# Opening a kernel's attention stage two products before its projections end

## The chip, the cores and the metric

The kernel runs on one core of a Trainium2 chip. The metric is the time of one execution on the device, in microseconds (us). A core has five engines that run their own instruction queues in order and wait for one another by semaphores: TensorE (PE in the profile; PEld is its weight load), VectorE (DVE), ScalarE (ACT), GpSimd (POOL) and SyncE (SP, which here only issues DMAs). TensorE writes its sums into PSUM, a small memory of eight banks; the other engines work from SBUF, the large on-chip memory, and carry the sums out of PSUM.

## The reference

One layer of a transformer trunk on 2048 tokens of width 1024, in float32:

```
h = rms_norm(x, g_pre_mix)
q, k, v = split_heads(h, w_qkv)                      # 16 heads of 64
for each chunk c of 64 tokens:                       # sees its own chunk and the 8 before
    sc  = q_c @ k_band^T / 8 + bias                  # bias: learned, clipped relative position
    o_c = softmax(sc) @ v_band
x = x + rms_norm(merge(o) @ w_o, g_post_mix)
h = rms_norm(x, g_pre_ffn)
x = x + rms_norm((silu(h @ w_gate) * (h @ w_up)) @ w_down, g_post_ffn)
```

## The kernel before

**Numbers.** Each float32 operand of a dense product is split into a rounded part ("hi") and the rest ("lo"), and three matmuls stand for one product (`products`, L197 to L199). ScalarE makes hi by a copy that rounds, VectorE makes lo by a subtraction (`split`, L356 and L357).

**Projections.** `project` (L1333) works in two groups `g` of 1024 tokens. Each dense product is a block scheme with seven products instead of eight, named in the order B11, B21, T1, T2, B22, T3, T4 (`BLOCKS`). In each group come first the values (`values_of`), then the queries and keys (`queries_keys`), four times (`c`) seven products of 24 matmuls, each product in two halves `i` (0 is the queries' half, 1 the keys'). In `values_of`, `put` adds a sum from PSUM to a stored term on VectorE (L1241), and `emit_v` (L426) scales the result by its token's inverse root on ScalarE (L428) and stores it. In `queries_keys`, the closing of a half is a sum on VectorE (L1305) and `emit_qk` (L431): a multiplication by the row of inverse roots (L436, VectorE), the hi part (L438, ScalarE), the lo part (L439, VectorE), and the stores to DRAM on SP.

**Scratch.** hi and lo take their tiles from `narrow`, which is `scratch` (L238): four tiles of 512 columns in a pool that always lives (`xp`) and, while the projections' pool `fp` is open, three more (`tmp`), in turn. A tile that still waits for its store to land holds up whoever takes it next. Tiles named `hb0` to `hb6` hold a group's block operands (`hb_tile`); in the second group `hb0` holds T3's operand.

**Attention.** 32 jobs `Attend(n, p)`: a quarter of 512 tokens `n` (in the order 1, 0, 2, 3) and a pair of heads `p`, with four slots of 128 queries each. A slot is: `scores` (L517), matmuls into the banks `st` (L533, L534), one reduction of each head on VectorE that adds the bias and finds the row's minimum (L542), one exponential on ScalarE (L546); `scaled` (L552), a reciprocal on VectorE and a multiplication by it on GpSimd (L558); `transposed` (L562), eight transposes on TensorE (L573) and copies out (L576 on VectorE, L578 on ScalarE); `fifth` (L587, L588). A job ends with `output`, the product with the values (L603). Scores run three slots ahead of transposes (`AHEAD`). The first quarter's eight jobs run alone; later ones have dense products between their slots. Job 0's operands are loaded during the projections (after T1 of the last `c`) into `hb2` and `hb3`; each later job has a `load` of its own on SP: two DMAs of queries, two of keys, four of biases, and for every second job two of values, into tiles of the pool `ap`. Job `j + 2` loads when the last scores of job `j` have been issued.

**Places and order.** `fp` and the projections' six PSUM banks (`psf`) are closed after the last product, and the attention's pools `ap`, `psa` and `pss` are opened on the same memory; two more banks (`ps`, tag `mm`) live throughout, and the first quarter's transposes use them. TensorE's order is the program's own; on the other engines the framework's planner chooses an order beforehand, by priority and by its own estimate of when each operand is ready, and each queue then runs in that order. `last_pool` and `last_sp` chain the DMAs of `weight_sums` (L842), which builds sums of weights in DRAM for the feed-forward part, behind the latest instruction of the queue that they go to: copies on SP (L852), accumulating DMAs on GpSimd (L856).

The transition, before the change:

```
drain()
stack_f[0].close()
... # ap, psa, pss opened; first_banks()
with tc.high_priority(offset=300):
    jobs[1].load()
for t in range(AHEAD):
    ahead(t)                    # scores of slot t
    if t < AHEAD - 1:
        jobs[0].scaled()
```

Of the kernel before, what the change touches and what calls it, by code (L numbers as in the profile page):

```python
# [9 lines left out]
F32 = mybir.dt.float32  # L10
F32R = mybir.dt.float32r
# [6 lines left out]
P = 128  # L18
# [31 lines left out]
def trunk(  # L50
# [195 lines left out]
    def narrow(name):  # L246
        return scratch(name)[:, :HALF]
# [156 lines left out]
    bias = {}  # L404

    bias_bufs = []

    def bias_tile(n, h, t=None):

# [13 lines left out]
            )  # L423
        return t

    def emit_v(n, m, u, t):  # L426

        act.activation(t, t, AF.Copy, scale=rs[n][:, m : m + 1])  # L428
        sp.dma_start(v_d[n][:, m, u * HALF : u * HALF + HALF], t)

    def emit_qk(n, p, which, src, t=None):  # L431

        scale = (0.125, 1.0)[which]
        if t is None:
            t = narrow("t")
        dve.tensor_tensor(t, src, rows_of[n], op=ALU.mult)  # L436
        hi, lo = (narrow(m).bitcast(F32R) for m in ("hi", "lo"))
        act.activation(hi, t, AF.Copy, scale=scale)  # L438
        dve.scalar_tensor_tensor(lo, t, scale, hi.bitcast(F32), op0=ALU.mult, op1=ALU.subtract)  # L439
        for a, part in enumerate((hi, lo)):  # L440
            part = part.bitcast(F32)
            if which == 0:
                sp.dma_start(q_d[n][p][:, a, :], part)
                continue
            for h, own in enumerate(heads):
                sp.dma_start(k_d[n][p][heads[a], h, :], part[own])
# [787 lines left out]
    def values_of(g, b, big):  # L1234

        s0, s1 = 2 * g, 2 * g + 1
        p1, z = ([big[:, 4 * n + m, :] for m in range(4)] for n in range(2))

        def put(n, m, u, a, b_, op=ALU.add):
            t = narrow("v")  # L1240
            dve.tensor_tensor(t, a, b_, op=op)  # L1241
            emit_v(n, m, u, t)

        def after(name, m, pt):
            if name == "B11":
                act.activation(p1[m], pt, AF.Copy)
            elif name == "B21":
                put(s0, m, 0, pt, p1[m])
            elif name == "T1":
                act.activation(z[m], pt, AF.Copy)  # L1250
            elif name == "T2":
                dve.tensor_tensor(p1[m], p1[m], pt, op=ALU.subtract)
                dve.tensor_tensor(z[m], z[m], p1[m], op=ALU.add)
            elif name == "B22":
                put(s1, m, 0, pt, z[m])
            elif name == "T3":
                dve.tensor_tensor(p1[m], pt, p1[m], op=ALU.subtract)
                put(s1, m, 1, pt, z[m], ALU.subtract)
            else:
                put(s0, m, 1, pt, p1[m])  # L1260

        for name in BLOCKS:
            b.need(name)
            w = [front.take() for _ in range(2)]
            begin = g == 0 and name == "B11"
            for part in [range(4)] if begin else [range(2), range(2, 4)]:
                pts = {m: bank("pv") for m in part}
                for m, k in [(m, k) for k in range(4) for m in part] if begin else [(m, k) for m in part for k in range(4)]:
                    tok = slice(m * P, m * P + P)
                    hi, lo = (t[:, k % 2 * HALF : k % 2 * HALF + HALF] for t in w[k // 2])  # L1270
                    products(pts[m], b.t[name][:, 0, k, tok], b.t[name][:, 1, k, tok], hi, lo, k == 0, k == 3)
                    yield 3 * C512
                    if k == 3:
                        after(name, m, pts[m])

    def queries_keys(g, b, big, after):

        def product(pts, name, first, then):
            hi, lo = front.take()
            for i in range(2):  # L1280
                for k in range(4):
                    c = slice(i * HALF + k * P, i * HALF + k * P + P)
                    products(
                        pts[i], hi[:, c], lo[:, c], b.t[name][:, 0, k, :], b.t[name][:, 1, k, :],
                        first and k == 0, k == 3, not first,
                    )
                    yield 3 * C512
                then(i)

        for c in range(NPAIR // 2):  # L1290
            at = 6 * (c % 2)
            p1, u2 = ([big[:, n + i, :] for i in range(2)] for n in (at, 4))
            p5 = [big[:, (2, 8)[c % 2] + i, :] for i in range(2)]
            s0, s1 = 2 * g, 2 * g + 1

            def copy(pts, dst):
                return lambda i: act.activation(dst[i], pts[i], AF.Copy)

            def u(i):
                dve.tensor_tensor(u2[i], p1[i], pb[i], op=ALU.subtract)  # L1300
                dve.tensor_tensor(p5[i], p5[i], p1[i], op=ALU.add)

            def closing(pts, terms, n, p, op=ALU.subtract):
                def go(i):
                    dve.tensor_tensor(terms[i], pts[i], terms[i], op=op)  # L1305
                    emit_qk(n, p, i, terms[i], terms[i])

                return go

            pa, pc = ([bank(n) for _ in range(2)] for n in ("pa", "pc"))  # L1310
            pb = []

            def t2():
                pb.extend(bank("pb") for _ in range(2))
                return pb

            steps = (
                ("B11", lambda: pa, True, copy(pa, p1)),
                ("B21", lambda: pa, False, lambda i: emit_qk(s0, 2 * c, i, pa[i])),
                ("T1", lambda: pc, True, copy(pc, p5)),  # L1320
                ("T2", t2, True, u),
                ("B22", lambda: pc, False, closing(pc, u2, s1, 2 * c, ALU.add)),
                ("T3", lambda: pb, False, closing(pb, p5, s1, 2 * c + 1)),
                ("T4", lambda: pb, False, closing(pb, p1, s0, 2 * c + 1)),
            )
            for name, pts, first, then in steps:
                yield from product(pts(), name, first, then)
                if c == NPAIR // 2 - 1:
                    after(name)

# [2 lines left out]
    def project():  # L1333
# [71 lines left out]
        for g in range(NG):  # L1405
            if g:
                big = xp.tile([P, 10, HALF], F32, tag="big", name="terms", bufs=1)
            yield from values_of(g, groups[g], big)
            drain()
            if g == 0:  # L1410
                later.extend(pause(20.0) + roots_by_tokens(2, 10.0, 12.0) + pause(8.0) + roots_by_tokens(3, 10.0, 12.0))

            def after(name, g=g):
                if g + 1 == NG:
                    if name == "T1":
                        jobs[0].load(True)
                    return
                if name == "B11":
                    now(build(1, "L11") + build(1, "L12"))
                elif name == "B21":  # L1420
                    now(build(1, "L21") + build(1, "L22"))
                elif name == "T1":
                    later.extend(timed((0.5, build(1, "B11", 1.8))))
                elif name == "T4":
                    later.extend(timed(
                        (0.5, build(1, "B21", 2.2)), (11.0, build(1, "T1", 2.5)), (24.0, build(1, "T2", 4.0)),
                        (42.0, build(1, "B22", 2.5)), (53.0, build(1, "T4", 2.5)), (64.0, build(1, "T3", 2.0)),
                    ))

            yield from queries_keys(g, groups[g], big, after)  # L1430

    def ffn():

# [115 lines left out]
    ctx.enter_context(tc.manual_schedule(engines={mybir.EngineType.PE}))  # L1549

    jobs = [Attend(n, p) for n in SEQ_OF for p in range(NPAIR)]
    open_ffn(0)
    sums_, done = weight_sums(), 0.0
    for c in project():
# [2 lines left out]
        if 350.0 < done and done % 8.0 < 1.0:  # L1557
            next(sums_, None)
    drain()
    stack_f[0].close()  # L1560
    phase.clear()

    phase["ap"] = stack_a.enter_context(tc.tile_pool(name="ap", bufs=2, reuse_waits="tile"))
    phase["psa"] = stack_a.enter_context(tc.tile_pool(name="psa", bufs=2, space=PSUM, reuse_waits="tile"))
    phase["pss"] = stack_s.enter_context(tc.tile_pool(name="pss0", bufs=2, space=PSUM, reuse_waits="tile"))
    first_banks()
    lates = [Late(o_d[n], POST_MIX, x[n], x1_d[n], n) for n in range(NQ)]
    work, owed, left = iter(()), [0.0], [0.0]

# [11 lines left out]

    slots = 4 * len(jobs)
    per = slots // NQ
    AHEAD = 3

    def ahead(t):
        if t == per:
            later_banks()
# [2 lines left out]
            if t % 4 == 3 and t // 4 + 2 < len(jobs):  # L1591
                jobs[t // 4 + 2].load()

    with tc.high_priority(offset=300):
        jobs[1].load()
    for t in range(AHEAD):
        ahead(t)
        if t < AHEAD - 1:
            jobs[0].scaled()
    for t in range(slots):  # L1600
        share = left[0] / max(per - t % per - 1, 1)
        if t > 0 and t % 4 == 0:
# [126 lines left out]
```

## Time and profile before

| | us |
|---|---|
| three timed runs | 2382.28, 2382.46, 2384.13; median 2382.46 |
| the profiled execution | 2379.12 |
| its span, first to last instruction | 2377.4 |
| TensorE busy in the span | 2325.9 (98%) |
| VectorE, ScalarE, GpSimd busy | 1636.7, 1149.6, 317.5 |
| end of the projections in the span | 476.45 |
| first output product of the attention | 501.82 |

A row of a timeline gives the start and the duration in us, the engine, the line of the kernel, the operation and its tiles (out<-in), the shape, and how many instructions were merged (x); in brackets stands how long the engine was idle before it, and what released it. Matmuls overlap their neighbours, so the distance between starts is what one costs. A row of a windows view gives, for a stretch of the span, its length, then each engine's busy time with its number of instructions, the clock granted to TensorE (1.00 is full), the share of time in which the DMA engines were busy, and GB/s. A row of a line's or tile's view gives minimum, median and maximum duration in ns and the first and last start. A row of DMA issues gives the number of issues, the size of one, and the median us from issue to landing; such rows here are from the window 440 to 500.

### The profile page before, as it was taken

How to read it: one execution, taken by the hardware profiler on the slowest of the kernel's cores; microseconds unless marked ns; L12 is line 12 of the kernel's file. 1: busy time of each engine (PE TensorE's matmuls, PEld its weight loads, DVE VectorE, ACT ScalarE, POOL GpSimd, SP SyncE). 2: the span in 40 equal slices, each digit the busy share in tenths (PEclk: the TensorE clock that was granted, in tenths of full speed). 3: DMA queues.
4: the chain of work that ended last, by engine and by line, in shares of the span. 5: the costliest groups of instructions: out<-in, count | busy, mean ns of one | idle time of the engine just before them, and what ended most of it. 6: DMA issues, size and time to landing. Idle time of an engine off the chain costs nothing.

```text
span 2377.4 us, 32908 instructions
## 1 busy us (share of the span) xinstructions
PE 2325.9 (98%) x11456; PEld 1908.3 (80%) x11456; DVE 1636.7 (69%) x2620; ACT 1149.6 (48%) x2031; POOL 317.5 (13%) x422
## 2 busy tenths in 40 slices
PE   8999999989999999999999999999999999999998
PEld 7888888878777777778888888888888888888886
DVE  7787856667566665669787877677667676555577
ACT  7544643367666565666333343455343333334454
POOL 1000011134333433420100000000000000000002
PEclk9999999999999999999999999999999999999999
DMA  8777899988897788765976463567665657447654
GB/s 298 255 254 264 246 276 270 288 235 225 220 257 214 248 253 239 227 226 204 288 262 210 158 213 138 186 221 248 221 217 190 221 162 234 149 158 244 193 187 148
DMA packets 231509, 531.80 MB, mean 224 GB/s; under 512 B 26512, under 2 KB 42912, under 8 KB 226864
## 3 DMA queue, kind: packets, MB, share of 16 engines
q1 hardware_dynamic: 219440, 482.52, 63.7%
q0 software_dynamic: 11904, 47.19, 7.0%
q8 instruction: 90, 1.47, 0.3%
q14 instruction: 75, 0.61, 0.1%
HBM read 382.23 MB, written 170.44 MB: 232 GB/s over the span
## 4 chain that ended last, share of the span: by engine, by line
PE 70%; DVE 2%; ACT 1%; issue 1%; DMA 0%; POOL 0%; DVEq 0%
PE pd L199 6%; PE pd L197 6%; PE pd L198 6%; PE pb L197 5%; PE pb L199 5%; PE pb L198 5%; PE tt L603 4%; PE pa L199 3%; PE pa L197 3%; PE pa L198 3%; PE pc L197 3%; PE pc L199 3%; PE pc L198 3%; PE tt L573 2%; PE mm L199 2%; PE mm L197 2%
## 5 line engine op out<-in xcount | busy, mean ns | idle before, releaser
L558 POOL TENSOR_SCALAR sc<-sc,rows 128x640 f32<-128x640 f32 (+4 forms) x256 | 194.9, 774 | 311.2 <-DVE rows L555 142.1
L546 ACT ACTIVATE sc<-sc,rows 128x640 f32<-128x640 f32 (+4 forms) x256 | 193.1, 757 | 75.9 <-DVE rows L542 75.0
L197 PE MATMUL pb<-hb,w_wg_T 128*128 128x512 f32 x528 | 205.9, 390 | 0.3
L199 PE MATMUL pb<-hb,w_wg_T 128*128 128x512 f32 x528 | 205.4, 389 | 0.0
L198 PE MATMUL pb<-hb,w_wg_T 128*128 128x512 f32 x528 | 205.4, 389 | 0.0
L542 DVE CUSTOM_DVE_ANT_0 sc<-st,bias 128x640 f32<-128x640 f32 (+2 forms) x248 | 174.6, 733 | 38.1 <-PE st L534 22.7
L533 PE MATMUL st<-k,q 128*128 128x384 f32 (+3 forms) x432 | 140.6, 342 | 25.4 <-DVE rows L542 21.5
L576 DVE COPY pT<-tt 128x512 f32<-128x512 f32 (+3 forms) x128 | 81.5, 637 | 101.2 <-PE tt L573 60.0
L199 PE MATMUL pd<-a,w_d_T 128*128 128x512 f32 (+1 forms) x368 | 139.9, 380 | 0.1
L197 PE MATMUL pd<-a,w_d_T 128*128 128x512 f32 (+1 forms) x368 | 139.9, 380 | 0.0
L198 PE MATMUL pd<-a,w_d_T 128*128 128x512 f32 (+1 forms) x368 | 139.8, 380 | 0.0
L197 PE MATMUL pa<-hb,w_wg_B 128*128 128x512 f32 x352 | 136.9, 389 | 0.0
L198 PE MATMUL pa<-hb,w_wg_B 128*128 128x512 f32 x352 | 136.9, 389 | 0.0
L199 PE MATMUL pa<-hb,w_wg_B 128*128 128x512 f32 x352 | 136.9, 389 | 0.0
L573 PEld LDWEIGHTS tt<-ident,sc 128*128 128x128 f32 x928 | 107.0, 142 | 34.6 <-issue 16.4
L131 ACT ACTIVATE w_wg_T<-raw 128x1024 fp32r<-128x1024 f32 x88 | 93.1, 1059 | 80.4 <-PE pa L199 37.7
L573 PE MATMUL tt<-ident,sc 128*128 128x128 f32 x928 | 127.2, 277 | 3.1 <-ACT pT L588 2.0
L534 PE MATMUL st<-k,q 128*128 128x384 f32 (+3 forms) x432 | 127.6, 315 | 0.0
L1027 ACT ACTIVATE terms<-terms 128x512 f32<-128x512 f32 x65 | 41.0, 631 | 173.1 <-DVE terms L1025 173.0
L289 POOL TENSOR_TENSOR rs<-ms,neg_half 128x4 f32<-128x4 f32 (+1 forms) x7 | 7.4, 1054 | 856.2 <-DVE ms L287 856.2
L603 PE MATMUL tt<-pT,v 128*64 128x512 f32 (+3 forms) x832 | 119.9, 436 | 0.1
L357 DVE TENSOR_TENSOR a<-raw_a,a 128x512 fp32r<-128x512 f32 x154 | 106.0, 694 | 19.0 <-ACT a L356 18.5
(274 smaller groups left out, 6207.5 us busy)
## 6 DMA issues: line engine op xcount, KB each, us to landing
raw<-in_w_gu SPq DMA_DIRECT2D x77, 512.0 KB, 4.2
q<-q SPq DMA_DIRECT2D x62, 512.0 KB, 6.5
k<-k SPq DMA_DIRECT2D x54, 512.0 KB, 8.0
s_g_S<-raw POOLq DMA_DIRECT2D x44, 512.0 KB, 3.1
raw_d<-d_S SPq DMA_DIRECT2D x88, 256.0 KB, 3.3
raw_a<-aT SPq DMA_DIRECT2D x88, 256.0 KB, 3.7
raw<-s_g_S SPq DMA_DIRECT2D x44, 512.0 KB, 4.1
bias<-ext_d SPq DMA_DIRECT2D x124, 144.0 KB, 8.4
```

The lines of the kernel that those rows point to most:

```text
L131: act.activation(hi, raw, AF.Copy)
L197: pe.matmul(pt, a_hi, b_hi, start=first, stop=False, skip_group_check=go_on)
L198: pe.matmul(pt, a_hi, b_lo, start=False, stop=False, skip_group_check=go_on)
L199: pe.matmul(pt, a_lo, b_hi, start=False, stop=last, skip_group_check=go_on)
L357: eng.tensor_tensor(lo, src, hi.bitcast(F32), op=ALU.subtract)
L533: pe.matmul(st[:, a:b], q[:, 2 * h, cols], kk[:, h, key], start=True, stop=False)
L534: pe.matmul(st[:, a:b], q[:, 2 * h + 1, cols], kk[:, h, key], start=False, stop=True)
L542: dve.tensor_tensor_reduce(out=sc[:, :n], in0=st[:, c0 : c0 + n], in1=rev, scale=-1.0, scalar=3.0e38, op0=ALU.add, op1=ALU.min, accum_out= ...
L546: act.activation(sc[:, :n], sc[:, :n], AF.Exp, bias=nmax, scale=-1.0, accum_out=rows[:, h : h + 1])
L558: last_pool[0] = pool.tensor_scalar(sc[:, :n], sc[:, :n], rows[:, 2 + h : 3 + h], 1.0, op0=ALU.mult, op1=ALU.mult)
L573: pe.transpose(tt[:, u, :], sc[h][:, b * P : b * P + P], ident)
L603: pe.matmul(po[heads[h], c0:c1], v[:, kb, c : c + 64], self.pT[:, h, r, c0:c1], start=m == 0, stop=m == len(terms) - 1,)
```

## The change

The attention's pools are now opened after B22 of the last `c` of the projections (`open_attention`, called by `after`), and job 1's loads are issued there. Slot 0's scores go behind the first half of T3, slot 1's behind its second half, slot 2's behind the first half of T4 (`during`); slots 0 and 1 are scaled right behind. T2's sums of that `c`, on which T3 and T4 go on, lie in the two `mm` banks instead of `psf`. The hi and lo parts of T4's two halves lie in four pieces of a new `hb0` (`emit_room`). And the four values of B21 in the first group are scaled by GpSimd instead of ScalarE.

```diff
-    def emit_v(n, m, u, t):
-        act.activation(t, t, AF.Copy, scale=rs[n][:, m : m + 1])
+    def emit_v(n, m, u, t, eng=act):
+        if eng is act:
+            act.activation(t, t, AF.Copy, scale=rs[n][:, m : m + 1])
+        else:
+            eng.tensor_scalar(t, t, rs[n][:, m : m + 1], 1.0, op0=ALU.mult, op1=ALU.mult)
         sp.dma_start(v_d[n][:, m, u * HALF : u * HALF + HALF], t)
...
-        hi, lo = (narrow(m).bitcast(F32R) for m in ("hi", "lo"))
+        hi, lo = ((emit_room.pop(0) if emit_room else narrow(m)).bitcast(F32R) for m in ("hi", "lo"))
...
             elif name == "B21":
-                put(s0, m, 0, pt, p1[m])
+                put(s0, m, 0, pt, p1[m], eng=act if g else pool)
...
                     yield 3 * C512
+                    if last:
+                        during(name, 4 * i + k)
                 then(i)
...
             def t2():
-                pb.extend(bank("pb") for _ in range(2))
+                if g + 1 == NG and c == NPAIR // 2 - 1:
+                    pb.extend(ps.tile([P, HALF], F32, tag="mm", name="pb") for _ in range(2))
+                else:
+                    pb.extend(bank("pb") for _ in range(2))
                 return pb
...
                     if name == "T1":
                         jobs[0].load(True)
+                    elif name == "B22":
+                        open_attention()
+                    elif name == "T3":
+                        flat = hb_tile(0, F32).rearrange("d s a c -> d (s a c)")
+                        emit_room.extend(flat[:, HALF * m : HALF * m + HALF] for m in range(4))
                     return
...
+            def during(name, m, g=g):
+                t = {("T3", 3): 0, ("T3", 7): 1, ("T4", 3): 2}.get((name, m))
+                if g + 1 == NG and t is not None:
+                    jobs[0].scores(t)
+                    if t < AHEAD - 1:
+                        jobs[0].scaled()
...
+    def open_attention():
+        drain()
+        stack_f[0].close()
+        phase.clear()
+        phase["ap"] = ...
+        phase["psa"] = ...
+        phase["pss"] = ...
+        first_banks()
+        with tc.high_priority(offset=300):
+            jobs[1].load()
...
-    with tc.high_priority(offset=300):
-        jobs[1].load()
-    for t in range(AHEAD):
-        ahead(t)
-        if t < AHEAD - 1:
-            jobs[0].scaled()
```

More of the change, by code (lines that the diff above doesn't have):

```diff
@@ L406, in trunk @@
     bias_bufs = []
+    emit_room = []
     def bias_tile(n, h, t=None):
@@ L1237, in values_of, with put @@
         p1, z = ([big[:, 4 * n + m, :] for m in range(4)] for n in range(2))
-        def put(n, m, u, a, b_, op=ALU.add):
+        def put(n, m, u, a, b_, op=ALU.add, eng=act):
             t = narrow("v")
             dve.tensor_tensor(t, a, b_, op=op)
-            emit_v(n, m, u, t)
+            emit_v(n, m, u, t, eng)
         def after(name, m, pt):
@@ L1274, in values_of, with queries_keys, product @@
                         after(name, m, pts[m])
-    def queries_keys(g, b, big, after):
-        def product(pts, name, first, then):
+    def queries_keys(g, b, big, after, during=lambda name, m: None):
+        def product(pts, name, first, then, last):
             hi, lo = front.take()
@@ L1326, in queries_keys @@
             for name, pts, first, then in steps:
-                yield from product(pts(), name, first, then)
+                yield from product(pts(), name, first, then, c == NPAIR // 2 - 1)
                 if c == NPAIR // 2 - 1:
@@ L1428, in after @@
                     ))
-            yield from queries_keys(g, groups[g], big, after)
+            def during(name, m, g=g):
[4 more added lines that the diff above has]
+                        jobs[0].scaled()
+            yield from queries_keys(g, groups[g], big, after, during)
     def ffn():
@@ L1551, in trunk @@
     jobs = [Attend(n, p) for n in SEQ_OF for p in range(NPAIR)]
+    AHEAD = 3
+    def open_attention():
+        drain()
+        stack_f[0].close()
+        phase.clear()
+        phase["ap"] = stack_a.enter_context(tc.tile_pool(name="ap", bufs=2, reuse_waits="tile"))
+        phase["psa"] = stack_a.enter_context(tc.tile_pool(name="psa", bufs=2, space=PSUM, reuse_waits="tile"))
+        phase["pss"] = stack_s.enter_context(tc.tile_pool(name="pss0", bufs=2, space=PSUM, reuse_waits="tile"))
+        first_banks()
+        with tc.high_priority(offset=300):
+            jobs[1].load()
     open_ffn(0)
@@ L1559, in trunk @@
     drain()
[L1560 to L1566, printed above, removed]
     lates = [Late(o_d[n], POST_MIX, x[n], x1_d[n], n) for n in range(NQ)]
@@ L1583, in trunk @@
     per = slots // NQ
-    AHEAD = 3
     def ahead(t):
```

## The prediction

> **What bounds the kernel.** The page's first part says which engine to follow, and the windows then say where it is not fed.
>
> ```profile
> PE 2325.9 (98%) x11456; PEld 1908.3 (80%) x11456; DVE 1636.7 (69%) x2620; ACT 1149.6 (48%) x2031; POOL 317.5 (13%) x422
> ```
> ```profile
> core 0: us, PE busy (x) PEld busy (x) DVE busy (x) ACT busy (x) POOL busy (x), PEclk, DMA share, GB/s
> 440.00:476.45 36.45, 36.45 (x162) 30.19 (x161) 20.12 (x28) 10.21 (x15) 3.32 (x14) 1.00 0.97 281
> 476.45:500.00 23.55, 16.25 (x87) 14.65 (x86) 14.84 (x35) 12.33 (x27) 6.30 (x8) 0.86 0.91 244
> 500.00:520.00 20.00, 19.48 (x141) 16.34 (x141) 12.34 (x35) 14.47 (x36) 10.20 (x13) 1.00 0.93 259
> ```
>
> TensorE is busy 98% of the span, so only what empties it counts. The projections end at 476.45 with no gap; then 23.55 us hold only 16.25 us of matmuls, at a granted clock of 0.86; after 500 it is fed again. TensorE's timeline shows that stretch, then an undisturbed job:
>
> ```profile
> 476.45 0.33 PE L533 MATMUL st<-hb 128*128 128x384 f32 x1
> ...
> 480.73 0.45 PE L533 MATMUL st<-hb 128*128 128x384 f32 x1 [2.48 <-DVE rows L542]
> ...
> 491.27 0.41 PE L533 MATMUL st<-k,q 128*128 128x384 f32 x1 [2.54 <-DMA k<-k]
> ...
> 492.94 0.52 PE L533 MATMUL st<-k,q 128*128 128x256 f32 x1 [1.08 <-DMA k<-k]
> ...
> 497.54 0.44 PE L533 MATMUL st<-k,q 128*128 128x384 f32 x1 [0.81 <-DVE rows L542]
> ...
> 501.82 4.63 PE L603 MATMUL tt<-pT,hb 128*64 128x512 f32 x32
> 506.38 1.09 PE L573 MATMUL tt<-ident,sc 128*128 128x128 f32 x8
> 507.23 0.42 PE L533 MATMUL st<-k,q 128*128 128x384 f32 x1
> ...
> 508.49 0.38 PE L587 MATMUL tt<-ident,sc 128*128 128x128 f32 x2
> ...
> 516.77 3.56 PE L603 MATMUL tt<-pT,hb 128*64 128x512 f32 x24
> ```
>
> From the end of T4 (476.45) to the first output product (501.82) are 25.37 us. The waits printed in these rows are 6.91 us, on VectorE (DVE) and on job 1's keys, and the granted clock of 0.86 is 0.14 x 23.55 = 3.3 us more. DVE's and SyncE's (SP) own rows explain both:
>
> ```profile
> 476.65 0.69 DVE L1305 TENSOR_TENSOR terms<-pb,terms 128x512 f32<-128x512 f32 x1 [1.30 <-PE pb L199]
> 477.26 0.68 DVE L439 SCALAR_TENSOR_TENSOR lo<-terms,hi 128x512 fp32r<-128x512 f32 x1
> ...
> 478.46 1.47 DVE L439 SCALAR_TENSOR_TENSOR lo<-terms,hi 128x512 fp32r<-128x512 f32 x2
> 479.85 0.82 DVE L542 CUSTOM_DVE_ANT_0 sc<-st,hb 128x640 f32<-128x640 f32 x1
> ```
> ```profile
> 470.62 1.69 SPq L72 DMA_DIRECT2D k<-lo  x2
> ...
> 481.45 1.31 SPq L72 DMA_DIRECT2D q<-q  x2
> ...
> 484.16 2.60 SPq L72 DMA_DIRECT2D bias<-ext_d  x4
> ...
> 490.12 1.47 SPq L72 DMA_DIRECT2D k<-lo  x2
> 492.91 1.29 SPq L72 DMA_DIRECT2D q<-q  x2
> ```
>
> Slot 0's scores lie ready at about 478, but DVE reduces them at 479.85, behind five operations of the last roundings, 0.6 us each; the low part at 477.26 is, by a count of the scratch tiles, that of T3's keys, whose tile still held a value of B22 on its way out. Job 1's loads are issued at 481.45 to 486.76, and TensorE waits for its keys until 492.94.
>
> **Opening the attention early.** The projections' end moves nowhere: by the first window's row a matmul takes 36.45 / 162 = 0.225 us and a product of 24 of them 5.4, so B22 ends at 465.6 and T3 at 471.0. The same matmuls run; what goes is waiting. One slot's scores take TensorE 508.49 - 507.23 = 1.26 us, so three slots inside T3 and T4 move T4's end to 480.2. An undisturbed stretch of four slots up to an output runs from 506.38 to 516.77, 10.39 us. The first output could start at 476.45 + 3.78 + 10.39 = 490.6 instead of 501.82: 11.2 us is the upper end. What comes off it:
>
> DVE. Inside T3 and T4 it has four closings of three operations (0.60 us apart in the rows above) and three slots' reductions of twice about 0.74: roughly 12 us over TensorE's 14.6 (5.4 for each product, 3.78 for scores), so it keeps up. But T4's second closing (1.8 us) can begin only when T4 ends, the transposes' second bank is one of T4's sums and is free only after its first operation, and the low part of T3's keys (0.6) is likely to stand there too. Those 2.4 us delay copies and reductions; the undisturbed stretch has idle time that takes up about 0.9. I take 1.5, between 0.5 (the bank alone) and 4.
>
> What the early opening itself waits for is short: the score banks and job 1's tiles lie where the projections' pool was, and its last reader is DVE taking B22's second sum, some 0.2 to 0.9 us after the product (476.65 after 476.45, 0.69 long); slot 0's scores come 2.7 us after it. Should that cover go, the first scores hold up T3's second half by the difference.
>
> ScalarE gets six exponentials beside four roundings, some 8 us in these 14.6, and was idle for most of them (10.21 busy of 36.45). GpSimd's scaling of slots 0 and 1 (two operations, 1.6 us a slot) has about 10 us until the first transposes, and the two accumulating DMAs of the weight sums that now must follow it are used only in the feed-forward part. Job 0's biases were issued from 456.93 on (below) and landed about 10.9 later, by about 470; slot 0's reduction comes at about 469.5: 0 to 0.5 us, taken in the 1.5.
>
> ```profile
> 456.93 3.46 SPq L72 DMA_DIRECT2D hb<-ext_d  x4
> ```
> ```profile
> k<-k SPq DMA_DIRECT2D x4, 512.0 KB, 8.9
> ...
> k<-lo SPq DMA_DIRECT2D x10, 128.0 KB, 4.0
> bias<-ext_d SPq DMA_DIRECT2D x8, 144.0 KB, 9.2
> ...
> hb<-ext_d SPq DMA_DIRECT2D x4, 144.0 KB, 10.9
> ```
>
> SP. Job 1's eight loads (5.3 us of issue; the four bias memsets on GpSimd with them are 0.14 each) move from 481 to about 466 to 475, past stores of T3 and T4; landing 9 later, they are there before slot 4 at about 484. Next in line is job 2's load: before, it began 492.91 and its scores ran at 507.23, 14.3 us later without a wait. After, those scores are wanted at about 497.5, and SP cannot begin before T4's last stores, about 484.5. That is 13.0 us, so I charge 1.0 (0 to 3).
>
> Contention. GpSimd's scaling now runs beside DVE operations with two operands in SBUF (L436, L439). In this trace such pairs lengthen each other:
>
> ```profile
> L265 DVE TENSOR_TENSOR osum<-osum,sq x20: 678/825/1620, 641.5 to 1034.7; 128x512 f32<-128x512 f32 x20
> ```
> ```profile
> 676.13 1.15 POOL L558 TENSOR_SCALAR sc<-sc,rows 128x384 f32<-128x384 f32 x2 [2.32 <-DVE rows L555]
> ...
> 695.95 1.36 POOL L558 TENSOR_SCALAR sc<-sc,rows 128x512 f32<-128x512 f32 x2 [3.99 <-ACT pT L578]
> ...
> 704.65 2.14 POOL L558 TENSOR_SCALAR sc<-sc,rows 128x384 f32<-128x384 f32 x2 [2.87 <-DVE rows L555]
> ```
>
> L265 takes 0.68 alone, 0.83 in the median, 1.62 at worst; the pair at 704.65 takes 1.0 longer than the one at 676.13. Two meetings at 0.25 each: 0.5 (0 to 2). Term: 11.2 - 1.5 - 1.0 - 0.5 = **8.2 us**, bounds 2.2 and 11.2. The separate tiles of T4's roundings, and T2's sums in the two spare banks, cost nothing by themselves: they let T4's roundings run without waiting for B22's stores.
>
> **Four values scaled by GpSimd.** Early on TensorE stands idle once for long:
>
> ```profile
> 47.10 0.80 PE L197 MATMUL pv<-w_wv_T,hb 128*128 128x512 f32 x1 [5.49 <-ACT hb L356]
> ...
> 71.81 0.50 PE L197 MATMUL pv<-w_wv_T,hb 128*128 128x512 f32 x1 [0.27 <-ACT hb L356]
> ```
> ```profile
> 43.98 2.54 ACT L428 ACTIVATE v<-v,hr 128x512 f32<-128x512 f32 x4
> 46.43 1.66 ACT L356 ACTIVATE hb<-hb 128x512 fp32r<-128x512 f32 x3
> ```
> ```profile
> 41.28 4.06 DVE L727 SCALAR_TENSOR_TENSOR hb<-hb,gt,hb 128x512 f32<-128x512 f32 x6
> 47.08 1.90 DVE L357 TENSOR_TENSOR hb<-hb,hb 128x512 fp32r<-128x512 f32 x3 [1.74 <-ACT hb L356]
> ```
>
> The four scalings (2.54 us) stand on ScalarE ahead of the rounding that T2 waits for; taken away, it comes up to 2.45 us earlier. But DVE works almost without a break from there to T3's start (71.81, which waits for roundings again), so TensorE cannot gain more there than DVE does: its 1.74 idle, and at most 0.9 elsewhere. Against it, GpSimd's four scalings (0.68 each, by the 128x512 pair above) fall among exactly these two-operand DVE operations: from 0 to 2.7 us lost. At 0.28 each I charge 1.1. Term: 1.74 - 1.1 = **0.6 us**, bounds -1.0 and 2.6. The values' stores, next on SP, were issued at 44.71 and nobody waits for them soon.
>
> **Sum.** 8.2 + 0.6 = 8.8 us. The profiled execution took 2379.12 (span 2377.4), so 2370.3 against that one; the three timed runs have median 2382.46, 3.3 above it, and I forecast their kind: **2373.7**.
>
> **Rivals.** *The keys' landing blocks DVE (slower).* T3 has only four scratch tiles once the projections' pool is closed, and counting the tiles out, the low part of T3's keys gets the one that holds B22's. Its store was issued at 470.62 to 472.31, landing 4.0 later, about 476.3; with job 1's eight loads ahead of it, it goes out 6 to 10 us later (before, the stores behind those loads left 6.2 to 10.1 us after 481.45), landing at 483 to 486. If DVE's order puts that rounding ahead of slot 1's reduction, due at about 474.5, DVE stands until the landing L and TensorE loses L - 474.5, and about 1.9 for the clock. It eats the 8.8 at L = 481.4 and is measurably slower from 486.2; at L = 487 the time is 2388. For it: SP is full there. Against it: in the trace the order held exactly this rounding back (477.26) until T4's sums had been taken.
>
> *The load stays late (same).* If SP's order keeps job 1's loads behind T4's stores, slot 4's keys land near 492.94 as now and the rest follows as before: only the 0.6 stays, 2381.9. For it: they stood late although marked urgent. Against it: their place is free early, since the bias tiles were filled at once:
>
> ```profile
> 460.36 0.14 POOL L416 MEMSET bias<- 64x64 f32 x1 [1.92 <-PE pb L199]
> ```
>
> *The slow clock isn't the waits' doing.* The 3.3 us of slow clock are counted as gone with the waits: the stretches before and after, with TensorE fed, have clock 1.00. If the clock falls for another reason, such as the step from long products to short scores, they come back: 2377.0. For it: no single wait in the rows is longer than 2.54 us. Against it: the window after 500 has the same short work at clock 1.00. The Trainium skill ("TensorE: Matmul & The Clock Gate", Part 1) has the clock halve only after about 3.4 us of idleness; by that, waits of at most 2.54 us would not do it, and the sum would be 5.5. The trace has clock 0.86 although no wait is that long, so I keep 8.8.
>
> **Chances.** Forecast 0.70, late load 0.10, slow clock 0.05, blocked DVE 0.15, of which 0.08 slower and 0.07 near zero. With the forecast's weak end (its terms at their lower bounds give 1.2 us) 0.03 goes to "same": faster 0.72, same 0.20, slower 0.08. About 0.2%, 4.8 us, is what a measurement can tell from no change. The range goes from both upper bounds, 2382.46 - 13.8 = 2368.7, rounded down for run noise, to 2380.5; it leaves out the late load's and blocked DVE's ends.
>
> **What would show it.** Right: the st matmuls of slots 0 to 2 stand between those of T3 and T4, no wait above 1 us before 501, granted clock 1.00 there, the first output near 492; the wait at 47.10 shorter, T3 a little earlier. Wrong: gaps inside T3 or T4 released by DVE rows or sc, a wait for k or bias at slots 4 or 8, DVE waiting on the landing of k stores, or L727 and L357 stretched beside GpSimd.

## The result, and the profile after

| | before | after |
|---|---|---|
| median of 22 runs each, on one chip | 2382.14 | 2377.13 |
| the profiled execution | 2379.12 | 2374.99 |
| its span | 2377.4 | 2373.2 |

The ratio is 0.9979, 95% interval 0.9973 to 0.9986: faster by 5.0 us, 3.3 to 6.4 by the interval; it leaves out one execution of each kernel that took far longer than all others. The forecast was 8.8 us. The other single executions lie up to 5 us from their kernel's median, so single positions in a trace are compared below, and medians only beside their intervals.

The windows of the changed kernel, in the same stretches as before:

```profile
core 0: us, PE busy (x) PEld busy (x) DVE busy (x) ACT busy (x) POOL busy (x), PEclk, DMA share, GB/s
440.00:476.45 36.45, 34.20 (x156) 28.34 (x155) 21.47 (x32) 11.21 (x18) 2.53 (x13) 1.00 0.99 277
476.45:500.00 23.55, 20.63 (x136) 17.55 (x134) 16.43 (x41) 14.58 (x36) 13.01 (x16) 1.00 1.02 293
500.00:520.00 20.00, 19.51 (x144) 16.99 (x142) 13.28 (x33) 14.09 (x33) 6.32 (x8) 1.00 0.86 231
```

TensorE is busy 20.63 us of the middle stretch instead of 16.25, at a granted clock of 1.00 instead of 0.86; in the first stretch it now lacks 2.25. Its timeline shows the waits that are left, and the first two outputs:

```profile
474.79 0.44 PE L537 MATMUL st<-hb 128*128 128x384 f32 x1 [2.25 <-DVE rows L546]
...
484.73 0.63 PE L577 MATMUL tt<-ident,sc 128*128 128x128 f32 x4 [1.27 <-POOL sc L562]
...
488.41 1.14 PE L577 MATMUL tt<-ident,sc 128*128 128x128 f32 x8 [1.64 <-ACT pT L582]
...
495.59 1.61 PE L607 MATMUL tt<-pT,hb 128*64 128x512 f32 x9
...
510.73 1.73 PE L607 MATMUL tt<-pT,hb 128*64 128x512 f32 x10
```

The first output comes at 495.59 instead of 501.82, 6.2 us earlier, and the second keeps that (510.73 against 516.77). Both waits for keys are gone; three others, 5.16 us together, stand in the opening. VectorE's rows tell why (the new lines: L1311 closing sum, L440 times the row, L443 low part, L546 reduction, L580 copy):

```profile
472.57 0.69 DVE L1311 TENSOR_TENSOR terms<-pb,terms 128x512 f32<-128x512 f32 x1 [0.99 <-PE pb L199]
473.30 0.69 DVE L440 TENSOR_TENSOR terms<-terms,row 128x512 f32<-128x512 f32 x1
473.91 0.82 DVE L546 CUSTOM_DVE_ANT_0 sc<-st,hb 128x640 f32<-128x640 f32 x1
...
482.90 1.08 DVE L443 SCALAR_TENSOR_TENSOR hb<-terms,hb 128x512 fp32r<-128x512 f32 x1 [0.36 <-ACT hb L442]
483.91 0.68 DVE L1311 TENSOR_TENSOR terms<-pb,terms 128x512 f32<-128x512 f32 x1
...
486.75 0.69 DVE L443 SCALAR_TENSOR_TENSOR hb<-terms,hb 128x512 fp32r<-128x512 f32 x1
...
488.09 0.69 DVE L580 COPY pT<-tt 128x512 f32<-128x512 f32 x1
```

- Slot 0's scores end by about 470, but VectorE idles 0.99 us for T3's second half, sums it and only then reduces slot 0 (473.91). Slot 1's scores need the banks: the 2.25 us wait.
- The transposes need a second bank. T4's second sum lies in it and is taken out at 483.91, behind a low part that lasts 1.08 instead of 0.69. GpSimd's scaling at 482.65 (below) runs beside that low part. TensorE's row names GpSimd, whose scaling ends at 484.65, but the sum ends at 484.59 and TensorE goes on 0.14 after it. The run e3 (below) separates the two: there the scaling lasts until 486.23, the row names the sum, and TensorE again goes on 0.14 after the sum's end at 485.76 (second row).
- The copies of slot 0 write `pT` into the tile that held T4's terms. The last reader of those is the low part at 486.75, ending 487.44; ScalarE's copy starts at 487.69, and TensorE's third wait ends with it.

```profile
482.65 2.00 POOL L562 TENSOR_SCALAR sc<-sc,rows 128x640 f32<-128x640 f32 x2 [0.88 <-DVE rows L559]
```
```profile
485.90 0.63 PE L577 MATMUL tt<-ident,sc 128*128 128x128 f32 x4 [0.44 <-DVE terms L1311]
```

SyncE's rows of the changed kernel, the loads of job 1 and of job 2:

```profile
471.60 1.31 SPq L72 DMA_DIRECT2D q<-q  x2
472.95 1.52 SPq L72 DMA_DIRECT2D k<-k  x2
...
488.67 2.38 SPq L72 DMA_DIRECT2D k<-hb  x4
491.10 1.97 SPq L72 DMA_DIRECT2D q<-q  x2
493.11 1.26 SPq L72 DMA_DIRECT2D k<-k  x2
```

Job 1's stand ten microseconds earlier than before (481.45); job 2's, behind T4's last stores (k<-hb), two (492.91). Early in the execution, by the timelines of TensorE, GpSimd and VectorE:

```profile
44.59 0.80 PE L197 MATMUL pv<-w_wv_T,hb 128*128 128x512 f32 x1 [2.59 <-ACT hb L356]
...
58.05 0.50 PE L199 MATMUL pv<-w_wv_B,hb 128*128 128x512 f32 x1 [1.05 <-DVE hb L357]
...
71.96 0.50 PE L197 MATMUL pv<-w_wv_T,hb 128*128 128x512 f32 x1 [1.09 <-ACT hb L356]
```
```profile
43.52 4.09 POOL L432 TENSOR_SCALAR v<-v,hr 128x512 f32<-128x512 f32 x4
```
```profile
44.57 2.48 DVE L357 TENSOR_TENSOR hb<-hb,hb 128x512 fp32r<-128x512 f32 x3 [1.39 <-ACT hb L356]
```

The wait at T2 is 2.9 us shorter, and T3 of the values starts 0.15 us later than before, not earlier. Of the 6.2 us that the first output gained, 4.2 are left at the end of the span. Two rows of this execution show waits that the kernel before does not have: one for the last job's keys (1017.96) and one for a closing in the feed-forward part (1167.11). VectorE, which makes that closing, had waited for a landing (`y<-o`) until 1155.48 and idles only 0.26 us from there on; before the change that wait ended at 1152.26 (last row).

```profile
1017.96 0.39 PE L537 MATMUL st<-k,q 128*128 128x256 f32 x1 [0.49 <-DMA k<-k]
```
```profile
1167.11 0.47 PE L197 MATMUL pb<-hb,w_wg_T 128*128 128x512 f32 x1 [1.18 <-DVE terms L1029]
```
```profile
1155.48 0.75 DVE L1213 SCALAR_TENSOR_TENSOR y<-y,gt,osum 128x512 f32<-128x512 f32 x1 [2.39 <-DMA y<-o]
```
```profile
1152.26 0.75 DVE L1209 SCALAR_TENSOR_TENSOR y<-y,gt,osum 128x512 f32<-128x512 f32 x1 [5.70 <-DMA y<-o]
```

The first of these waits is not where the loss comes from in general. e11, the same kernel once more, does not have it: the stretch from the output before those scores to the next one takes 19.96 us there, as before the change (20.90 in the execution above), and yet of 5.8 us gained at the first output 3.2 are left at the end.

### The profile page after: what moved, and what is told of

The parts are those of the page before. It is cut to its first block, busy times and chain, and to the rows that moved or that the text cites. A ratio compares the mean times of both kernels' runs of the same rounds, so it can differ in the third digit from the quotient of the medians.

```text
span 2373.2 us, 32914 instructions
## 1 busy us (share of the span) xinstructions
PE 2323.0 (98%) x11456; PEld 1903.4 (80%) x11456; DVE 1636.0 (69%) x2620; ACT 1145.5 (48%) x2027; POOL 322.8 (14%) x426
## 4 chain that ended last, share of the span: by engine, by line
PE 67%; DVE 3%; DMA 2%; ACT 1%; issue 1%; SPq 0%; POOL 0%; DVEq 0%
PE pd L199 6%; PE pd L198 6%; PE pd L197 6%; PE pb L197 5%; PE pb L199 5%; PE pb L198 5%; PE tt L607 3%; PE pc L197 3%; PE pc L199 3%; PE pa L199 3%; PE pa L197 3%; PE pc L198 3%; PE pa L198 3%; PE tt L577 2%; PE mm L199 2%; PE mm L197 2%
## 5 line engine op out<-in xcount | busy, mean ns | idle before, releaser
L546 DVE CUSTOM_DVE_ANT_0 sc<-st,bias 128x640 f32<-128x640 f32 (+2 forms) x248 | 174.5, 733 | 37.4 <-PE st L538 22.6
L580 DVE COPY pT<-tt 128x512 f32<-128x512 f32 (+3 forms) x128 | 81.5, 637 | 97.1 <-PE tt L577 55.8
```

Of the source, the lines that this page charges most:

```text
L546: dve.tensor_tensor_reduce(out=sc[:, :n], in0=st[:, c0 : c0 + n], in1=rev, scale=-1.0, scalar=3.0e38, op0=ALU.add, op1=ALU.min, accum_out= ...
```

## The experiments

The first theory: the early scores make the gain, three waits in VectorE's and ScalarE's orders take part of it, and the four values on GpSimd are worth nothing. Its rivals: the loads' place or the own tiles carry the gain; the values are worth 0.6. All edits are against the changed kernel. "To the first output" is the time from the first matmul of the last T3 (465.57 in the trace before, 465.75 after) to the first output product; it leaves out what earlier stages shift. Each ratio is to the kernel before, run on the same chip; e1 to e4 ran on one chip, e5 to e12 on another.

| | to the first output | second output after | ratio to before, interval |
|---|---|---|---|
| before | 36.25 | 14.95 | |
| after | 29.84 | 15.14 | 0.9979 (0.9973 to 0.9986) |
| e1 values by ScalarE | 31.45 | 15.14 | 0.9975 (0.9965 to 0.9985) |
| e2 scratch turn | 31.46 | 15.18 | 0.9978 (0.9970 to 0.9987) |
| e3 no own tiles | 35.02 | 14.34 | 0.9995 (0.9986 to 1.0005) |
| e4 scores behind T4 | 30.64 | 15.42 | 0.9972 (0.9962 to 0.9982) |
| e5 job 1's loads behind | 39.23 | 14.31 | 1.0019 (1.0009 to 1.0029) |
| e6 e3 and e4 | 35.31 | 14.35 | 0.9991 (0.9982 to 0.9999) |
| e7 own sums | 28.49 | 15.14 | 0.9978 (0.9968 to 0.9987) |
| e8 scores earlier | 29.93 | 15.17 | 0.9971 (0.9960 to 0.9982) |
| e9 e7 and e8 | 28.95 | 20.05 | 0.9977 (0.9966 to 0.9988) |
| e10 e4 and e7 | 30.18 | 15.45 | 0.9971 (0.9959 to 0.9983) |
| e11 after, again | 29.88 | 15.16 | 0.9977 (0.9967 to 0.9986) |
| e12 e9, job 2's loads earlier | 28.12 | 17.72 | 0.9984 (0.9974 to 0.9993) |

**e1: the values scaled by ScalarE again.**

```diff
-                put(s0, m, 0, pt, p1[m], eng=act if g else pool)
+                put(s0, m, 0, pt, p1[m])
```

> The changed kernel with one part undone: the four values of B21 are scaled by ScalarE again. Theory (the stretch before T3 is bounded by VectorE, and GpSimd's work beside it costs what it saves): PE waits at T2 for 5.5 us instead of 2.6, the waits in B22 and at T3 (2.9 us together in the changed kernel) go, the three VectorE operations of the low parts take 1.9 us again instead of 2.48, T3 of the values starts at 71.8 to 72.1, and the time stays at 2377.1 within 0.5. Rival (the prediction's 0.6 us for this part): T3 starts near 72.6 and the time is 2377.7. Second rival (GpSimd costs more than it saves): T3 before 71.5.

T2 waits 5.80 us again, the low parts take 1.89, the waits in B22 are gone, and T3 starts at 72.41, between the theory's 72.1 and the rival's 72.6. But T3 starts anywhere from 71.89 to 72.74 in the traces with GpSimd's scaling, and at 71.81 in the trace before, without it. The ratio, 0.9975 against 0.9979, does not move beyond its interval, which is wider than 0.6 us. So no worth of this part is shown, and 0.6 us is not excluded. The 1.6 us more to the first output are the clock, which after the same 2.25 us wait fell here and not in the changed kernel's profile (more of this at e11).

**e2: the turn of the scratch tiles.**

```diff
     drain()
+    turn[0] += 4
```

> The changed kernel with the turn of the scratch tiles moved on by four after the projections, so that the later stages take the same tiles as before the change (the four own tiles of T4's roundings took four turns out). Theory (the 1.18 us wait of PE on VectorE's closing terms at 1167.1 us, new in the changed kernel, comes from the shifted turn): that wait is gone, the offset to the kernel before stays at 5.0 us from 1098 to 1552 us of the trace instead of falling to 4.0, and the time is about 2376.0. Rival (the wait is a chance of that one execution's transfers): the wait may or may not show, the time stays at 2377.1.

The wait at 1167 is gone: from the norm's sums of the first part of the feed-forward stage (`pssq`) to those of the second it is 71.41 us, as before (1130.63 to 1202.04), against 72.83 in the changed kernel. But from there to the third it is 1105.02 against 1103.21 in the changed kernel and 1103.58 before, and the median stays (2376.84). So the missing gain is not the turn's doing. Nor does the turn alone decide the row at 1167: e8, with the turn of the changed kernel, takes 71.48 for the first stretch. What else that wait depends on stays open.

**e3: T4's roundings in scratch tiles; e4: the scores behind T4; e6: both.**

```diff
-                    elif name == "T3":
-                        flat = hb_tile(0, F32).rearrange("d s a c -> d (s a c)")
-                        emit_room.extend(flat[:, HALF * m : HALF * m + HALF] for m in range(4))
```
```diff
-                t = {("T3", 3): 0, ("T3", 7): 1, ("T4", 3): 2}.get((name, m))
+                t = None
...
+    for t in range(AHEAD):
+        jobs[0].scores(t)
+        if t < AHEAD - 1:
+            jobs[0].scaled()
     for t in range(slots):
```

> The changed kernel with T4's four roundings in the rotating scratch tiles again. Theory (own tiles matter in the opening: the low part of T4's queries would take the tile of T3's low queries, whose store is issued at 477.5 behind job 1's loads and lands some 8 us later): VectorE waits up to 2.7 us there, the first output of attention starts between 495.6 and 498.3 (495.59 with own tiles), and, since the turn of the scratch tiles is that of the kernel before again, the wait at 1167 goes (-1.2): 2375.9 to 2378.6. Rival (own tiles do nothing in the opening, the planner only puts that operation elsewhere): first output at 495.6 within 0.3, and 2375.9.

> The changed kernel with pools, job 1's loads and own tiles where the change puts them, but the three slots' scores behind T4 as before the change. Theory (the scores' place carries the gain): the first output starts at 501 to 503, the PE clock falls below 1.00 again between 476 and 500 us, and the time is 2382 to 2384. Rival (the pools' and loads' early opening carries it): first output near 496, and 2377.

> Both undone: the scores behind T4, and T4's roundings in the rotating scratch tiles; pools and job 1's loads stay early. Theory (the own tiles matter wherever the scores stand: T4's low parts wait for a scratch tile in VectorE's order, and the transposed copies of slot 0 write the tile in which T4's terms lie until the last low part has read them): first output at 499 to 502 and 2379 to 2382, as with own tiles undone alone. Rival (own tiles matter only for scores inside T3 and T4): 496.6, as with the scores behind alone, and 2375.5.

e4 contradicts the first theory. With the scores where they were before the change, the first output comes 0.8 us later than in the changed kernel's two traces, which have a full clock there, and 0.8 earlier than in e1 and e2, whose clock falls as much as e4's (e4: 0.87 from 480 to 484 and 0.71 from 484 to 488). With own sums in both, e10 comes 1.7 later than e7, where only e10 has a slow clock, which costs it as much (0.74 and 0.83 in the same windows). The ratios, 0.9972 for e4 and 0.9971 for e10, are no worse than those of the changed kernel and of e7. So no gain of the early scores themselves is shown. TensorE's waits of e4 are those of slots 1 and 2, and no wait for keys is left:

```profile
480.74 0.44 PE L537 MATMUL st<-hb 128*128 128x384 f32 x1 [2.51 <-DVE rows L546]
...
482.83 0.62 PE L537 MATMUL st<-hb 128*128 128x384 f32 x1 [0.49 <-DVE rows L546]
...
492.37 0.44 PE L537 MATMUL st<-k,q 128*128 128x384 f32 x1 [0.93 <-DVE rows L546]
```

So the early scores bring three waits (5.16 us) in place of these (3.93 us and a slow clock). e3 and e6 show what the gain hangs on. Without own tiles the first output is 4.7 us later with the scores behind (e6 against e4) and 3.6 later with them inside (e3 against e1 and e2, whose clock falls in the same window as e3's); e3 lost more than was expected of it. By the ratios it is 4.5 us (e6 against e4), clear of the intervals, and 3.8 (e3 against the changed kernel), where the intervals touch. In e6, TensorE's row, VectorE's rows and ScalarE's:

```profile
491.49 1.94 PE L577 MATMUL tt<-ident,sc 128*128 128x128 f32 x8 [6.53 <-ACT pT L582]
```
```profile
487.87 0.71 DVE L443 SCALAR_TENSOR_TENSOR lo<-terms,hi 128x512 fp32r<-128x512 f32 x1 [0.88 <-DMA q<-lo]
...
489.96 0.69 DVE L443 SCALAR_TENSOR_TENSOR lo<-terms,hi 128x512 fp32r<-128x512 f32 x1 [1.38 <-ACT hi L442]
```
```profile
489.28 0.63 ACT L442 ACTIVATE hi<-terms 128x512 fp32r<-128x512 f32 x1 [2.49 <-DMA k<-hi]
```

The first low part waits for a scratch tile, and the second for ScalarE's hi part, which waits for another. The stores of both tiles stand on SP behind job 1's early loads: q<-lo is issued at 480.04 and lands 7.8 us later, k<-hi follows from 483.47. Until the last low part has run, the copies of slot 0 may not write the terms' tile, and TensorE stands for 6.53 us; behind that wait the clock is 0.50 from 492 to 496, which is part of the difference. In e3 the same copy ends a wait of 4.05 us. There q<-lo lands 9.4 us after 478.94, but the low parts run only at 489.88, behind slot 3's reductions and exponentials and with no idle time for a store in their rows, so in e3 the planned order has a share that no run separates. The early loads make T4's roundings late, and the own tiles pay that back.

**e5: job 1's loads behind T4's stores.**

```diff
-        with tc.high_priority(offset=300):
-            jobs[1].load()
...
         job.transposed(t % 4)
+        if t == 0:
+            jobs[1].load()
```

> The changed kernel with one thing moved: job 1's loads are issued behind T4's stores again, as before the change (scores, pools and own tiles stay). Theory (the early place of job 1's loads, which the early pools allow, carries about half of the 6.2 us at the first output): TensorE waits for k<-k at slot 4 again, 2 to 4 us beyond the 489 us at which it needs them, first output at 498 to 501, time 2380 to 2382. Rival (the transfer is hidden in any case, the scores' place carries the gain): first output 495.6 to 497.6, time 2377.

The loads stand behind slot 0's transposes here and have lost their priority. Job 1's keys are issued at 489.98, some 7 us later than before the change and 17 later than in the changed kernel. TensorE's rows, and its clock after them:

```profile
494.85 0.66 PE L537 MATMUL st<-k,q 128*128 128x384 f32 x1 [3.97 <-DMA k<-k]
...
497.69 0.58 PE L537 MATMUL st<-k,q 128*128 128x256 f32 x1 [1.87 <-DMA k<-k]
```
```profile
492.00:496.00 4.00, 0.98 (x2) 0.50 (x2) 0.00 (x0) 0.00 (x0) 0.84 (x2) 0.50 0.98 305
496.00:500.00 4.00, 2.31 (x10) 2.31 (x11) 0.83 (x2) 0.00 (x0) 0.00 (x0) 0.50 1.05 238
```

With scores and own tiles in place, this alone makes the kernel slower than before: 2386.79 at a ratio of 1.0019, with the first output 9.4 us later than in the changed kernel. The size is more than expected, since the keys came out later than before the change. Loads and own tiles belong together: to the first output e6, which has the early loads and not the tiles, is 0.9 us better than before, and e4, which has both, is 5.6 better. Own tiles with the loads issued exactly where they were before the change were not run, so the share of the loads alone is not measured.

**e7: T4's sums in own tiles too; e8: the scores half a product earlier; e9: both; e10: e7 with e4's scores.**

```diff
+        if emit_room:
+            t = emit_room.pop(0)
-        if t is None:
+        elif t is None:
             t = narrow("t")
...
-                        emit_room.extend(... for m in range(4))
+                        emit_room.extend(... for m in range(6))
```
```diff
-                t = {("T3", 3): 0, ("T3", 7): 1, ("T4", 3): 2}.get((name, m))
+                t = {("T3", 1): 0, ("T3", 6): 1, ("T4", 2): 2}.get((name, m))
```

> The changed kernel with two more own tiles: T4's two sums times the row go to tiles of their own too, so that the tile that holds T4's terms, which the transposed copies of job 0 overwrite, is read for the last time one rounding earlier. Theory (TensorE's third wait of the opening, 1.64 us on ScalarE's copy at 488.41, ends with the last low part of T4 at 487.44 and not with slot 3's exponential): that wait falls to 0 to 0.4, the first output comes 1.2 to 1.6 earlier than in an execution of the changed kernel with the same clock (494.2 against 495.59, or 496.2 against 497.6), time 2375.7. Rival (the copy stands behind the exponential of slot 3): the wait stays at 1.6, time 2377.1.

> The changed kernel with the three slots' scores earlier by two blocks, one block and one block of T3 and T4 (slot 0 behind T3's block 1, slot 1 behind T3's block 6, slot 2 behind T4's block 2), by which VectorE's order takes slot 0's reduction ahead of T3's second sum. Theory (TensorE's first wait of the opening, 2.25 us at 474.79, is the reduction standing behind that sum): it falls to 0.6 to 1.3, no fall of the granted clock follows between 476 and 480, first output 494 to 495, time 2375.5. Rival (VectorE's work only changes places, its total in the stretch sets the end): a wait of the same size comes later in T4, first output 495.6 to 497.6, time 2377.

> The changed kernel with both edits that shortened one wait each: the scores half a product earlier and T4's sums in own tiles. Theory (the waits add): TensorE's waits of the opening are 1.7 and 1.3 to 1.5 us, the third is gone; first output near 494.0 with the clock at 1.00, 1.5 before the changed kernel's 495.6; time 2375 to 2376. Rival (what is gained before the first output is given back later, at the last job's keys near 1018 us and by chance falls of the clock): first output 494.0 all the same, time 2377 to 2378.

> The changed kernel with the three slots' scores behind T4 and T4's sums in own tiles. Theory (with the scores behind T4 VectorE ends the roundings before slot 0's reduction, so no copy waits for the terms' tile and the own sums change nothing): the waits stay at 2.5, 0.5 and 0.9 us with the clock near 0.7 from 484 to 488, first output 496.6, time 2375.5 to 2377. Rival (own sums take 1.3 us off there too): first output 495.3.

e7 settles the third wait: it is gone and the first output comes 1.35 us earlier, so its cause is the tile that the copies overwrite. The planner then also puts ScalarE's copy ahead of slot 3's exponential (486.72 and 488.32). In the changed kernel the exponential ahead of it cannot account for more than 0.25 us: the tile was held until 487.44 and the copy ran at 487.69. The median (2377.99) does not show the gain. e8 shortens the first wait from 2.25 to 1.66 us only, the second grows to 1.52, and the first output does not move (29.93); VectorE's work there changes places. e10 is e4 within 0.5 us. e9 has the two waits of e8 without the third (0.77 in place of 1.52 for the second, and a slow clock before it), and then loses 5 us between the first two outputs:

```profile
505.07 0.41 PE L539 MATMUL st<-k,q 128*128 128x384 f32 x1 [1.90 <-DMA k<-k]
...
506.58 0.58 PE L539 MATMUL st<-k,q 128*128 128x256 f32 x1 [0.89 <-DMA k<-k]
```
```profile
508.00:512.00 4.00, 4.00 (x19) 4.00 (x18) 2.37 (x6) 2.56 (x6) 0.00 (x0) 0.50 1.06 212
```

Job 2's keys are late, and the clock falls to a half behind that wait. The transfers' part of the profile has the landing of these two loads as its last number, in the changed kernel (issues from 493 to 495 us) and then in e9 (493 to 496):

```profile
k<-k SPq DMA_DIRECT2D x2, 512.0 KB, 7.1
```
```profile
k<-k SPq DMA_DIRECT2D x2, 512.0 KB, 11.7
```

They were issued at 493.11 in the changed kernel and at 493.68 in e9, and wanted at 503.48 and 503.17; e7, which wanted them at 502.90, does not wait (they landed 7.5 after their issue). So it is the landing that was late in this execution and not the opening that was too early for it. It is not a single case, since job 2's keys took 11.3 us in e3 and 11.5 in e5; why they take longer in some executions stays open. The waits add at the first output (28.95 with a slow clock, 28.12 in e12 without one); the time does not follow.

**e11: the changed kernel once more.**

> The changed kernel itself, once more. Its first profile has the 2.25 us wait at 474.79 and the clock at 1.00 behind it; three variants with the same wait have 0.57 to 0.58 from 476 to 480 and come 2.0 us later to the first output. Theory (whether the clock falls after that wait is chance, not a matter of the edit): one execution can show either, first output 495.6 or 497.6 (within 0.8 for the start), the rest alike; time 2377.1. Rival (those variants' edits cause the fall): clock 1.00 and 495.6 again.

The window behind the 2.25 us wait, in e1 and then in e11:

```profile
476.00:480.00 4.00, 4.00 (x13) 3.32 (x13) 2.40 (x7) 2.71 (x8) 2.08 (x3) 0.57 1.02 229
```
```profile
476.00:480.00 4.00, 4.00 (x21) 3.50 (x21) 2.61 (x8) 2.73 (x8) 2.49 (x4) 1.00 1.03 240
```

Full clock again, so the run does not show by itself that the same kernel can do either. But e5 and e7 have the wait and 1.00 as well, and e1, e2 and e3 have 0.57 to 0.58, where e1's and e2's edits lie far from the place. Behind the 1.66 us wait it is 0.73 in e9 and 1.00 in e8 and e12. Chance fits this better than the edits do; it is not proved. The chip is a rival that these runs leave open: e1, e2 and e3 ran on one, e5, e7 and e11 on the other. Only the 1.66 us wait has both outcomes on one chip.

**e12: e9 with job 2's loads during T4.**

```diff
                     if t < AHEAD - 1:
                         jobs[0].scaled()
+                    if t == 1:
+                        jobs[2].load()
...
-            if t % 4 == 3 and t // 4 + 2 < len(jobs):
+            if t % 4 == 3 and 3 <= t // 4 + 2 < len(jobs):
```

> The kernel with the scores half a product earlier and T4's sums in own tiles, and with job 2's loads issued during T4, ahead of T4's stores (they read what earlier pairs stored). Theory (job 2's keys, issued at 493.68 and waited for at 505.07 and 506.58 with the clock at 0.50 behind it, are what the earlier opening runs into): no wait for k<-k before 520, second output 15.1 to 15.3 after the first instead of 20.0, first output 493.5 to 495.1, time 2373 to 2375. Rival (the transfers crowd out others: job 1's keys or the stores land later): first output 496 or later, time 2377 or more.

No keys are waited for and the first output is the earliest of all (493.82, 28.12 after T3's start), but the second comes 17.72 later, not 15.1 to 15.3:

```profile
511.54 3.68 PE L609 MATMUL tt<-pT,hb 128*64 128x512 f32 x12 [3.37 <-DVE hb L616]
```
```profile
502.36 2.53 SPq L72 DMA_DIRECT2D k<-hb  x4
```

VectorE's L616 rounds the first output into a tile of the set on which T4's own tiles lie, and T4's stores now go out at 502.36 instead of 488.67. That the rounding is late for these stores is argued from the shared tile and not shown. By its rows ScalarE's part of it (L615, at 510.15) waits for nothing: it stands in the planned order behind exponentials that keep ScalarE busy from 501.42, and the stores land 3.3 us after their issue, by about 508. The time is 2379.27; no version here beats the changed kernel by more than the intervals.

## Why the prediction was right, and where not

The direction and the stage were right, and 2377.13 lies in the range, which is 11.8 us wide; the gain was 5.0 us instead of 8.8. The hit owes something to that width: the sum credits the early scores, for which no gain is shown, puts too little on VectorE's order, and has nothing for what later stages give back.

- **Opening, 8.2 us.** To the first output 6.4 were gained. The upper end, 11.2, holds in the same terms: 36.25 before, and T3, T4, three slots' scores and an undisturbed stretch make 25.0. The step that failed is the deduction of 3.0; the changed kernel is 4.8 above that floor.
- **DVE, 1.5 of it.** This is the term that was mis-sized: the three waits are 5.16 us. The second bank (1.27) was foreseen. That "it keeps up" was not true of the order: slot 0's reduction stood behind T3's second sum (2.25 us, where the prediction had only 0 to 0.5 for job 0's biases), and the tile that copies and T4's terms share (1.64) was not in the prediction.
- **Job 2's load, 1.0.** It cost nothing in the changed kernel, whose opening came 5 us later than the 490.6 on which the charge rested: the two terms were not independent. The margin is thin: in e9, where these keys landed 4.6 us later, TensorE waits 2.79 us for them.
- **Contention, 0.5.** The pair of scalings at 482.65 took 2.00 us, where the same pair takes 1.57 in e3, and the low part 1.08 instead of 0.69: 0.8 us together, near the term, and part of the second wait.
- **Own tiles "cost nothing by themselves".** True, and the reason given, that T4's roundings need not wait for stores, is what the gain hangs on (e3, e6: 3.6 to 4.7 us). The prediction counted them as a condition and the scores' place as the source. By e4 the latter is worth 0.8 us at a full clock in the changed kernel and -0.8 at a slow one in both, and nothing by the ratios.
- **Four values, 0.6 us.** Not seen (e1). The bound by VectorE was right; GpSimd's four operations took 4.09 us instead of the 2.7 expected, the three low parts 2.48 instead of 1.90, and the waits at 58.05 and 71.96 gave back what T2 gained.
- **Not foreseen:** 2 us given back later, in this execution 0.9 at the last job's keys (the stretch from the output at 1007.76 to 1028.66 takes 20.90 instead of 19.96) and about 1.1 in the feed-forward part. e11 gives back 2.6 without the former, so where it goes varies, and the cause stays open.
- **Two slips in its sums** change nothing here: the upper bound of 11.2 leaves out the 0.5 that is the least of DVE's term, and the weak end of 1.2 us would be 2381.3 and not the range's 2380.5.
- **The rivals.** Keys' landing: no such stall, T3's last low part ran at 475.39 without a wait (in e7 it waits 0.40 us); its mechanism, stores behind the early loads, is real for T4's roundings (e3, e6). Load stays late: it did not, but e5 shows that its place decides the sign. Slow clock: its 2377.0 is next to the measured 2377.13, but only by chance, since with 2.91 us of waits left from 476.45 to 500 the clock there is 1.00. In e1, e2 and e3 it does fall, from 476 to 480. The Trainium skill ("TensorE: Matmul & The Clock Gate", Part 1) has a free-running window of about 3.4 us that must be idle before the clock halves. A free-running window agrees with falls that come in some executions only; the length does not, since the clock fell to 0.57 behind waits of 2.25 us.

## What to carry to other kernels

Moving work earlier pays through what it lets start, here transfers, and those push others back in the same queue: look up which stores stand behind the moved loads and who needs their tiles, and give these tiles of their own. Work put into another stage runs in the order of the engine that serves both, so count for each step what stands ahead of it there, not only the engine's sum. When several parts are needed together, undoing one at a time shows each as if it carried the whole gain; undo two at once before crediting either.

## What the hardware showed

- The granted clock behind one wait of TensorE, in windows of 4 us: behind 1.66 us it was 0.73 in one execution of three (e9; not e8, e12); behind 2.25 us 0.57 to 0.58 in three of seven (e1, e2, e3, all on one chip; not after, e5, e7, e11); behind 2.48 to 2.51 us 0.71 to 0.87 in all three (before, e4, e10); behind 3.37 to 6.53 us it reached 0.50 in all four (e3, e5, e6, e12). In e1 and e2 the fall cost 1.6 us to the first output, as much as some of the edits.
- Four 128x512 scalings on GpSimd took 4.09 us, 1.02 each, beside VectorE operations with two operands in SBUF, which took 2.48 instead of 1.90 for three.
- Job 2's keys, two loads of 512 KB, landed 7.1 to 7.9 us after their issue in four traces (after, e7, e8, e11) and 11.3 to 11.7 in three (e3, e5, e9).
